# A two-layer mixer kernel: its steps in another order, keys scaled out of PSUM beside the values, small products held among large ones, the output projection begun with the heads' half

## The chip, the cores and the metric

One core of a Trainium2 chip runs the whole program in one launch. The metric is the device time of that launch in microseconds (us). The kernel before was timed three times; the median stands in the table below. Engines: PE is TensorE (PEld its weight loads), DVE is VectorE, ACT is ScalarE, POOL is GpSimd, SP is SyncE, which issues most of the DMAs. PSUM is the memory that PE writes its results to; here it is used in eight banks, two to each of four pools (pi, pa, pb, pc).

## The reference, cut to what matters

Everything is float32. Two layers of 512 tokens by 1024 features, each of four steps:

```python
h <- LN(alpha*h + 0.5*SwiGLU_a(h))
h <- LN(alpha*h + W_o [GDN | SB | MLA](h))     # the mixer
h <- LN(alpha*h + 0.5*SwiGLU_b(h))
h <- h + sigmoid(h W_g) * (p[i] W_p)
```

Only the mixer changes. It multiplies h by one wide in-projection and feeds three groups of heads. GDN (gated delta rule, 8 heads of 64) works in chunks of 64 tokens. For each chunk and head it needs the inverse of a 64 by 64 lower triangular matrix, applied to two right sides:

```python
lhs = strict_lower(einsum(kb, kc) * decay) + eye(C)
u = triangular_solve(lhs, vc * bc)                # values times beta
w = triangular_solve(lhs, kb * exp(gc))           # keys times beta and decay
v_new = u - w @ state;  o = q_dec @ state + qk @ v_new
state = state * g_last + k_dec.T @ v_new
```

The output of GDN is normalised and multiplied by silu of a gate gz. SB (stick-breaking attention, 4 heads) and MLA (latent attention, 4 heads, low-rank queries and keys) are attentions over the 512 tokens. The 1024 features of the three groups go through W_o.

## The kernel before, in words

**Large products.** A float32 product is made of three matmuls on split operands (a high part and a low part, `fp32r`): `mm3`, lines 408 to 410. Each has a full 128 by 128 weight tile and 256, 416 or 512 columns; these are called large here. The weights come by DMA (SP), ACT casts the high part (L78) and POOL or DVE subtracts it to get the low part (L80), three weights ahead.

**Small products.** The chunk algebra uses plain float32 matmuls on small corners of the array: tiles of 16 or 32 rows in the inverse, of 64 rows in the products of a chunk.

**The mixer's steps.** A string of names per layer, `OPT[l]["order"]` (L31 and L35), says in which order the steps are written: `k`, `q`, `v`, `si` are in-projections of 128 columns of keys, queries, values and of the stick heads, `pr` the key products of a chunk pair, `inv0` to `inv2` the inverse of the 16 by 16 corners (on DVE: L928 to L957), `in2` and `in3` the corners joined to 32 and 64 (small products on PE, L970 to L1003), `keys` the transposed keys, `lat_in` the latent in-projection, `lh` the latent heads, `dq` the decayed queries, `uw` the products u and w, `mv` the moves of a chunk, `sc` the scan over chunks, `st` the stick attention, `la` and `lo` the latent attention, `gz` the gate, `on` and `go` its norm and product. A scheduler then sets each engine's queue from this order and from when it takes operands to be ready. Each engine works its queue strictly in order.

**u and w.** `u_w(t)` first multiplies the inverse EA by the values (L1022, 64 columns for each head and chunk), ACT copies u out of PSUM (L1023), POOL scales EA by a number per token (L647), PE multiplies the scaled EA by the keys (L1029), ACT copies w (L1030), and POOL scales the keys (L647 on K). `moves(t)` (L1050 and after) needs w and the scaled keys.

**Values.** `in_values` transposes silu of the convolved values y (L870) and scales them out of PSUM (L871); the convolution is three DVE instructions (L839), the product with silu's second factor one more (L667).

**Output projection.** After all steps, the gate is transposed, and then four groups of 24 large matmuls of 512 columns make the first column half of the output, for which four banks are held; the heads of SB and MLA fill one half of the 1024 input features, GDN's the other.

Of the kernel before, what the change touches and what calls it, by code (L numbers as in the profile page):

```python
# [30 lines left out]
    {"order": "gates_in gates q1 si3 si0 k0 k3 si1 decays si2 q2 st03 st02 k1 st01 q3 k2 st00 q0 scales pr2 pr0 st13 st12 st11 st10 pr3 lw pr1 inv0 inv1 inv2 v1 v0 lat_in in2 v3 v2 keys dm lh0 in3 lh3 dq lh2 qs lh1 uw0 mv0 uw1 mv1 uw2 mv2 uw3 mv3 gz0 gz1 la00 la10 lo0 la01 la11 lo1 mxa sc0 sc1 sc2 sc3 la02 la12 lo2 on0 go0 on1 go1 on2 go2 on3 go3 la03 la13 lo3",  # L31
     "units": "MXl SQK EA KS SPb LO K KT KQ1 GZ MXh KQ0 SVM QT V EU MW MGh MGl SPa IA",
     "out": (2, 1, 0, 3),
# [3 lines left out]
     "out": (2, 1, 0, 3),  # L37
     "eng": {"EAm": "V", "EUm": "V", "gu": "V", "sil_max": "G", "sil_mul": "V", "by_EA": "G", "by_K": "G", "gnw": "G", "gout": "G", "mxlo": "G", "new": "G", "splo": "G", "pscale": "V", "c_sphi": "A", "c_stq": "V", "c_pT1": "V", "c_pT0": "A", "c_mo": "A", "c_K": "V", "c_u": "A", "c_w": "A", "c_o": "A", "c_vm": "A", "c_kv": "V", "c_qv": "A", "c_rv": "A", "c_mqT": "A", "c_QKT": "A", "c_mxhi": "A", "c_gz": "A", "c_kt": "A", "c_sv": "A", "r_lnf": "G", "r_lnm": "G", "r_m": "G", "r_k": "V", "r_o": "V", "lnf_g": "V", "lnf_b": "V", "lnm_g": "G", "lnm_b": "V", "f_T": "V", "f_Tlo": "G", "f_S": "V", "f_Slo": "V", "f_c": "G", "f_S3": "V", "f_T3": "G", "c_pj": "V", "sel": "V", "w_gates": "G", "w_si": "V", "w_k": "G", "w_q": "V", "w_v": "G", "w_lat": "G", "w_gz": "G", "w_o0": "G", "w_o1": "G", "s_gates": "G", "s_si": "V", "s_k": "V", "s_q": "V", "s_v": "G", "s_lat": "V", "s_gz": "G", "s_o0": "V", "s_o1": "V"}},
# [78 lines left out]
def trunk(  # L117
# [249 lines left out]
    def plan_mixer(l):  # L367
# [13 lines left out]
        plans = {"gates_in": p_gates, "lat_in": p_lat, "gz0": lambda: p_gz(0), "gz1": lambda: p_gz(1)}  # L381
# [3 lines left out]
        for st in opt["order"].split():  # L385
            if st in plans:
                plans[st]()
# [18 lines left out]
    def mm3(ps, ah, al, bh, bl, first, last):  # L406

        T.matmul(ps, ah, bh, start=first, stop=False)  # L408
        T.matmul(ps, ah, bl, start=False, stop=False)  # L409
        T.matmul(ps, al, bh, start=False, stop=last)  # L410
# [209 lines left out]
    def mixer(l):  # L620
# [9 lines left out]
        def cols(dst, w):  # L630
            for k in range(KD):
                mm3(dst, w[0][:, k * P:(k + 1) * P], w[1][:, k * P:(k + 1) * P], XH[:, k, :], XL[:, k, :], k == 0, k == KD - 1)

        def col_tile():
            w = W.next()
            ps = ibank()
            cols(ps, w)
            return ps

        def tok_tile(ps, t, ws, n, per):  # L640
            for k in range(KD):
                u, kk = k // per, k % per
                mm3(ps, XH[:, k, t * P:(t + 1) * P], XL[:, k, t * P:(t + 1) * P],
                    ws[u][0][:, kk * n:(kk + 1) * n], ws[u][1][:, kk * n:(kk + 1) * n], k == 0, k == KD - 1)
# [32 lines left out]
        KS, LO, Vt = U["KS"], U["LO"], U["V"]  # L677
# [59 lines left out]
        def in_latent():  # L737
            ws = [W.next() for _ in range(4)]
            for t in range(NT):
                ps = ibank()  # L740
                tok_tile(ps[:, 0:416], t, ws, 416, 2)
                CP["kt"](KT[:, t, 0:416], ps[:, 0:416])
# [56 lines left out]
        lo = {}  # L799

        def latent(h2, qt):
            N = (qt + 1) * P
            if qt not in lo:
                lo[qt] = slab("lo", 256)
            for hp in range(2):
# [6 lines left out]
                p_, pT = (MW[:, hp, :N], MW[:, 2 + hp, :N]) if h2 == 0 else (SVM[:, hp, :N], SQK[:, 2 + hp, :N])  # L812
# [50 lines left out]
        def in_values(ct):  # L863
            if True:
                y, e = slab("y"), slab("e")
                conv(col_tile(), 8 + ct, y)
                silu(y, e)
                pv = bank()
                for t in range(NT):
                    T.transpose(pv[:, t * P:(t + 1) * P], y[:, t * P:(t + 1) * P], ident)  # L870
                V.tensor_tensor(out=Vt[:, :, ct * P:(ct + 1) * P].rearrange("p t (h d) -> p t h d", h=2), in0=pv.rearrange("p (t h d) -> p t h d", t=NT, h=2),  # L871
                                in1=th(brk)[:, :, 2 * ct:2 * ct + 2].unsqueeze(3).broadcast_to([P, NT, 2, 64]), op=ALU.mult)
# [17 lines left out]
        def decayed_queries():  # L890
# [3 lines left out]
            eh, el = LO[:, 2, :], LO[:, 3, :]  # L894
            sel = tp.tile([P, 512], F32R, tag="t", name=nm("sel"))
# [68 lines left out]
        def inverse32():  # L964
            DN, QZ = inv_s["DN"], inv_s["QZ"]
            pq = bank()
            for n in range(32):
                for q in range(4):
                    R, o = quad(q)
                    T.matmul(pq[R, n * 16:(n + 1) * 16], LC[R, n, :], DT[R, n, 16:32], start=True, stop=True)  # L970
            A.copy(QZ[:, :, 16:32], pq.rearrange("p (n i) -> p n i", i=16))
            pe_, pn = bank(), one()
            for n in range(32):
                for q in (1, 3, 0, 2):
                    R, K16 = slice(32 * q, 32 * q + 32), slice(32 * q, 32 * q + 16)
                    T.matmul(pe_[R, n * 16:(n + 1) * 16], DN[K16, n, :], QZ[K16, n, 16:32], start=True, stop=True)
                    if q % 2 == 0:
                        T.matmul(pn[R, n * 16:(n + 1) * 16], QZ[K16, n, :], DN[K16, n, 0:16], start=True, stop=True)
# [7 lines left out]
        def inverse64():  # L986
            DN, TS = inv_s["DN"], inv_s["QZ"]
            pt = banks()
            for n in range(32):
                for cp in range(2):  # L990
                    R = slice(cp * 64 + 32, cp * 64 + 64)
                    T.matmul(pt[n // 16][cp * 64:cp * 64 + 32, (n % 16) * 32:(n % 16) * 32 + 32], EAf[R, n, 0:32], EAf[R, n, 32:64], start=True, stop=True)
# [7 lines left out]
            for n in range(32):  # L1000
                for cp in range(2):
                    R = slice(cp * 64, cp * 64 + 32)
                    T.matmul(py[n // 16][R, (n % 16) * 32:(n % 16) * 32 + 32], DN[R, n, :], TS[R, n, :], start=True, stop=True)  # L1003
# [6 lines left out]
        def keys():  # L1010
            for ct in range(4):
                pk = bank()
                for t in range(NT):
                    T.transpose(pk[:, t * P:(t + 1) * P], kq(ct, 0)[:, t * P:(t + 1) * P], ident)
                CP["K"](K[:, :, ct * P:(ct + 1) * P], pk.rearrange("p (t c) -> p t c", t=NT))

        def u_w(t):
            pu = bank()
            for hh in range(8):
                for cp in range(2):  # L1020
                    R = slice(cp * 64, cp * 64 + 64)
                    T.matmul(pu[R, hh * 64:(hh + 1) * 64], EA[R, t, hh * 64:(hh + 1) * 64], Vt[R, t, hh * 64:(hh + 1) * 64], start=True, stop=True)  # L1022
            CP["u"](Vt[:, t, :], pu)  # L1023
            by_token(EN["by_EA"], EA[:, t, :], EA[:, t, :], cw2, t)
            pw = bank()
            for hh in range(8):
                for cp in range(2):
                    R = slice(cp * 64, cp * 64 + 64)
                    T.matmul(pw[R, hh * 64:(hh + 1) * 64], EA[R, t, hh * 64:(hh + 1) * 64], K[R, t, hh * 64:(hh + 1) * 64], start=True, stop=True)  # L1029
            CP["w"](EA[:, t, :], pw)  # L1030
            by_token(EN["by_K"], K[:, t, :], K[:, t, :], kd, t)
# [10 lines left out]
        def moves(t):  # L1042
            pa = banks()
            for hh in range(8):
                h2, hp = hh // 2, hh % 2
                for cp in range(2):
                    R = slice(cp * 64, cp * 64 + 64)
                    Rh, c = slice(hp * 64, hp * 64 + 64), slice(hh * 64, (hh + 1) * 64)
                    for w_, rhs in ((0, K), (1, EU)):
                        T.matmul(pa[cp][Rh, w_ * 256 + h2 * 64:w_ * 256 + (h2 + 1) * 64], EA[R, t, c], rhs[R, t, c], start=True, stop=True)  # L1050
# [5 lines left out]
            for cp in range(2):  # L1056
                R = slice(cp * 64, cp * 64 + 64)
                pb = bank()
                for hh in range(8):
                    h2, hp = hh // 2, hh % 2  # L1060
                    T.matmul(pb[hp * 64:hp * 64 + 64, h2 * 64:(h2 + 1) * 64], K[R, t, hh * 64:(hh + 1) * 64], Vt[R, t, hh * 64:(hh + 1) * 64], start=True, stop=True)
# [259 lines left out]
```

## Time and profile before

| | us |
|---|---|
| median of three runs | 2320.2 (2308.31 to 2324.55) |
| the profiled execution | 2316.84 |
| its span | 2315.1 |
| PE busy | 2254.1 (97%) |
| DVE, ACT, POOL busy | 1310.1 (57%), 1059.9 (46%), 854.9 (37%) |

The profile is of one execution. The two mixers run from about 370 to 765 us and from about 1520 to 1910 us of its span. In a row of a timeline the first number is the start, the second the time in the engine. Matmuls are pipelined: how long one keeps PE is read from the start of the next, not from its own second number. In rows of plain float32 products, one product of the program shows as two instructions. PEclk is the clock granted to PE as a share of the full 2.4 GHz; the lower level is 1.2 GHz.

### The profile page before, as it was taken

How to read it: one execution, taken by the hardware profiler on the slowest of the kernel's cores; microseconds unless marked ns; L12 is line 12 of the kernel's file. 1: busy time of each engine (PE TensorE's matmuls, PEld its weight loads, DVE VectorE, ACT ScalarE, POOL GpSimd, SP SyncE). 2: the span in 40 equal slices, each digit the busy share in tenths (PEclk: the TensorE clock that was granted, in tenths of full speed). 3: DMA queues.
4: the chain of work that ended last, by engine and by line, in shares of the span. 5: the costliest groups of instructions: out<-in, count | busy, mean ns of one | idle time of the engine just before them, and what ended most of it. 6: DMA issues, size and time to landing. Idle time of an engine off the chain costs nothing.

```text
span 2315.1 us, 41403 instructions
## 1 busy us (share of the span) xinstructions
PE 2254.1 (97%) x17362; PEld 2001.4 (86%) x17362; DVE 1310.1 (57%) x1988; ACT 1059.9 (46%) x1751; POOL 854.9 (37%) x467
## 2 busy tenths in 40 slices
PE   8999999999989999999999999999999899999999
PEld 8999888767777999988889998887687789999887
DVE  7777416655435877642567774165553558777233
ACT  5555423653443555532345554236535445556222
POOL 4222452432334422255432225524334244223442
PEclk9999999998899999999999999999999899999999
DMA  5332342212103233234313323422120033333331
GB/s 170 101 105 91 115 125 63 60 38 59 47 21 89 76 110 101 82 119 128 122 44 108 101 93 110 128 56 67 37 77 23 20 92 97 104 102 98 112 101 64
DMA packets 186795, 199.94 MB, mean 86 GB/s; under 512 B 10128, under 2 KB 151536, under 8 KB 186608
## 3 DMA queue, kind: packets, MB, share of 16 engines
q1 hardware_dynamic: 186608, 197.29, 28.2%
q8 instruction: 136, 2.23, 0.4%
q14 instruction: 51, 0.42, 0.1%
HBM read 195.17 MB, written 2.10 MB: 85 GB/s over the span
## 4 chain that ended last, share of the span: by engine, by line
PE 90%; DVE 4%; POOL 2%; issue 2%; ACT 1%; DMA 1%; SPq 0%; POOLq 0%; DVEq 0%; ACTq 0%
PE pi L408 6%; PE pi L409 6%; PE pi L410 6%; PE pc L414 4%; PE pc L416 4%; PE pc L415 4%; PE pa L416 3%; PE pa L415 3%; PE pa L414 3%; PE pb L416 3%; PE pb L415 3%; PE pb L414 3%; PE pb L408 3%; PE pb L410 3%; PE pc L410 3%; PE pc L408 3%
## 5 line engine op out<-in xcount | busy, mean ns | idle before, releaser
L80 POOL TENSOR_TENSOR wlo<-wraw,whi 128x1024 fp32r<-128x1024 f32 (+4 forms) x169 | 351.5, 2089 | 407.7 <-ACT whi L78 399.6
L78 ACT CAST whi<-wraw 128x1024 fp32r<-128x1024 f32 (+2 forms) x162 | 167.0, 1033 | 346.0 <-PE pa L410 166.1
L100 POOL TENSOR_TENSOR wlo<-wq,whi 128x1024 fp32r<-128x1024 f32 x48 | 121.4, 2529 | 291.6 <-ACT whi L99 291.6
L99 ACT CAST whi<-wq 128x1024 fp32r<-128x1024 f32 x116 | 121.7, 1049 | 131.8 <-issue 37.7
L100 POOL TENSOR_TENSOR wlo<-wraw,whi 128x1024 fp32r<-128x1024 f32 x32 | 82.2, 2568 | 234.6 <-ACT whi L99 186.5
L99 ACT CAST whi<-wraw 128x1024 fp32r<-128x1024 f32 x84 | 88.1, 1049 | 96.2 <-issue 25.8
L414 PE MATMUL pb<-x,whi 128*128 128x256 f32 x448 | 127.0, 286 | 2.5 <-ACT x L255 1.7
L415 PE MATMUL pb<-x,whi 128*128 128x256 f32 x448 | 127.3, 286 | 0.0
L414 PE MATMUL pc<-x,whi 128*128 128x256 f32 x448 | 126.8, 283 | 0.4 <-ACT sg L184 0.4
L100 DVE TENSOR_TENSOR wlo<-wq,whi 128x1024 fp32r<-128x1024 f32 x68 | 84.5, 1243 | 75.4 <-ACT whi L99 75.4
L416 PE MATMUL pb<-x,wlo 128*128 128x256 f32 x448 | 127.1, 286 | 0.0
L415 PE MATMUL pc<-x,whi 128*128 128x256 f32 x448 | 126.8, 283 | 0.0
L416 PE MATMUL pc<-x,wlo 128*128 128x256 f32 x448 | 126.7, 283 | 0.0
L99 ACT CAST whi<-s 128x1024 fp32r<-128x1024 f32 x80 | 83.9, 1049 | 69.5 <-PE pc L415 40.1
L100 DVE TENSOR_TENSOR wlo<-s,whi 128x1024 fp32r<-128x1024 f32 x80 | 106.8, 1335 | 0.0
L409 PE MATMUL pi<-x,whi 128*128 128x512 f32 x256 | 104.9, 410 | 0.7 <-issue 0.7
L410 PE MATMUL pi<-x,wlo 128*128 128x512 f32 x256 | 104.4, 408 | 0.0
L408 PE MATMUL pi<-x,whi 128*128 128x512 f32 x256 | 104.2, 407 | 0.0
L100 DVE TENSOR_TENSOR wlo<-wraw,whi 128x1024 fp32r<-128x1024 f32 x52 | 65.6, 1261 | 57.1 <-ACT whi L99 57.1
L416 PE MATMUL pa<-x,wlo 128*128 128x256 f32 x320 | 91.8, 287 | 2.8 <-DVE wlo L100 2.8
L414 PE MATMUL pa<-x,whi 128*128 128x256 f32 x320 | 91.5, 286 | 0.0
L415 PE MATMUL pa<-x,whi 128*128 128x256 f32 x320 | 91.5, 286 | 0.0
(575 smaller groups left out, 7698.2 us busy)
## 6 DMA issues: line engine op xcount, KB each, us to landing
wq<-in_ffa_w_in_dram SPq DMA_DIRECT2D x46, 512.0 KB, 3.7
wq<-in_ffb_w_in_dram SPq DMA_DIRECT2D x46, 512.0 KB, 3.8
wraw<-in_ffa_w_out_dram SPq DMA_DIRECT2D x44, 512.0 KB, 3.7
wraw<-in_ffb_w_out_dram SPq DMA_DIRECT2D x44, 512.0 KB, 3.7
wraw<-in_mix_w_in_dram SPq DMA_DIRECT2D x40, 512.0 KB, 3.8
wraw<-in_ffa_w_in_dram SPq DMA_DIRECT2D x34, 512.0 KB, 3.6
wraw<-in_ffb_w_in_dram SPq DMA_DIRECT2D x34, 512.0 KB, 4.0
wraw<-in_mix_w_o_dram SPq DMA_DIRECT2D x16, 512.0 KB, 3.7
```

The source lines that it names most:

```text
L78: self.nc.scalar.copy(hi[:, :width], raw[:, :width])
L80: (eng or self.nc.gpsimd).tensor_tensor(out=lo[:, c], in0=raw[:, c], in1=hi[:, c].bitcast(F32), op=ALU.subtract)
L99: nc.scalar.copy(hi, q[name])
L100: eng(name).tensor_tensor(out=lo, in0=q[name], in1=hi.bitcast(F32), op=ALU.subtract)
L408: T.matmul(ps, ah, bh, start=first, stop=False)
L409: T.matmul(ps, ah, bl, start=False, stop=False)
L410: T.matmul(ps, al, bh, start=False, stop=last)
L414: T.matmul(dst, ah, bhl[:, 0], start=first, stop=False, skip_group_check=True)
L415: T.matmul(dst, ah, bhl[:, 1], start=False, stop=False, skip_group_check=True)
L416: T.matmul(dst, al, bhl[:, 0], start=False, stop=last, skip_group_check=True)
```

## The change

The order string of both layers is new; `pr` and the inverse come right after `scales`, all four `v` come before `in2`, and the latent in-projection is cut into `lat0` to `lat3`, of 24 large matmuls each. A step written `in2~lat0,lat1` is woven: the function of the small products yields after each of its 64 groups, and a large matmul of the named steps, from the seventh on, is ordered behind a group in proportion (no semaphore, an order for the scheduler only). `gz0 gz1` come before `uw0`.

`keys` makes the transposes by token tile and evicts each bank twice, scaled: once into VK beside the values, once into K. `u_w` then needs one stage: EA times (value, scaled key) pairs of 128 columns. Values are scaled out of PSUM in two instructions in place of one. The gate has its tiles in the two tags of the layer norm's parameters, so the loads of these (`ln_load`) come behind the gate's transposes. Of the output projection the half on the heads of SB and MLA comes ahead of the gate's transposes, and the first half's banks are two of pi, and one each from two other calls.

```diff
-"... st00 q0 scales pr2 pr0 st13 st12 st11 st10 pr3 lw pr1 inv0 inv1 inv2 v1 v0 lat_in in2 v3 v2 keys dm lh0 in3 lh3 dq lh2 qs lh1 uw0 mv0 uw1 mv1 uw2 mv2 uw3 mv3 gz0 gz1 la00 ..."
+"... q0 scales pr2 pr0 pr3 pr1 inv0 inv1 inv2 st00 si3 si1 v1 st13 v0 st12 v2 st11 v3 st10 lw in2~lat0,lat1 keys dm lh0 in3~lat2,lat3 dq lh1 gz0 gz1 uw0 mv0 lh2 qs uw1 mv1 lh3 uw2 mv2 uw3 mv3 la00 ..."
...
-                CP["K"](K[:, :, ct * P:(ct + 1) * P], pk.rearrange("p (t c) -> p t c", t=NT))
+                by_token(V, VK[t][:, 1, :], pk, cw2, t)
+                by_token(V, K[:, t, :], pk, kd, t)
...
-            CP["u"](Vt[:, t, :], pu)
-            by_token(EN["by_EA"], EA[:, t, :], EA[:, t, :], cw2, t)
...
-            CP["w"](EA[:, t, :], pw)
-            by_token(EN["by_K"], K[:, t, :], K[:, t, :], kd, t)
+            for i in range(2):
+                pu = bank()
...
+                        T.matmul(pu[R, hh * P:(hh + 1) * P], EA[R, t, c], VK[t][R, :, c], start=True, stop=True)
+                CP["w" if i else "u"](VK[t][:, :, i * 256:(i + 1) * 256].rearrange("p w (h d) -> p h w d", h=4), pu.rearrange("p (h w d) -> p h w d", h=4, w=2))
...
+        def woven(gen, fill):
+            n, done = sum(96 if f[:2] == "gz" else 24 for f in fill), [0]
+            small_ = []
+            def turn(i):
+                done[0] += 1
+                if done[0] > 6 and (done[0] - 6) * 64 // n < len(small_):
+                    tc.add_manual_dep(i.ins, small_[(done[0] - 6) * 64 // n].ins.name, NOSYNC, reason="among the small products")
+                while len(small_) < 64 and len(small_) * n < done[0] * 64:
+                    small_.append(next(gen))
...
-        ps0 = banks4()
+        ps0 = [ibank(), ibank(), one(True), one(True)]
         ws = [W.next() for _ in range(4)]
         for t in range(NT):
             for i in range(2):
                 mm_o(ps0[t], t, order[i], ws[i], i == 0, False)
+        regroup("silu_and_others")
...
+        ln_load(l, 1)
...
-        pb = banks() + banks(True)
+        pb = banks() + [bank(), bank()]
```

The pieces below are of the engines' queues; a name's number tells buffers apart, `x128` is so many instructions in a row.

PE, layer 1, the first products of `in2` (`pa<-IA`) with the large matmuls about them (`pi`: before those of a value step, 512 columns; in the change those of `lat0`). Before:

```order
L408 MATMUL pi_5450<-x_3498,whi_4992 128x512
L970 MATMUL pa_5112<-IA_3702 32x16 x128
L409 MATMUL pi_5450<-x_3498,whi_4992 128x512
L410 MATMUL pi_5450<-x_3498,wlo_4993 128x512
L408 MATMUL pi_5498<-x_3498,whi_4998 128x512
```

In the change:

```order
L410 MATMUL pi_5108<-whi_4991,x_3498 128x416
L975 MATMUL pa_5110<-IA_3702 32x16 x4
L408 MATMUL pi_5108<-whi_4991,x_3498 128x416
L975 MATMUL pa_5110<-IA_3702 32x16 x8
L409 MATMUL pi_5108<-wlo_4992,x_3498 128x416
L975 MATMUL pa_5110<-IA_3702 32x16 x4
```

One block of 128 has become groups of 4 or 8 with a single large matmul between; `in3` looks the same. In layer 1 small products of the inverse follow a large matmul at 78 places of the new queue and at 4 of the old one.

DVE, layer 1, the end of the corners' inverse (`IA`, `DN`) and what stands about it. Before:

```order
L945 TENSOR_TENSOR IA_3702<-pr_4832,pa_4833 128x30
L946 TENSOR_TENSOR pa_4833<-pa_4833,IA_3702 128x2x15
L956 STREAM_TRANSPOSE IA_3702<-X_4872 128x32x32
L957 STREAM_TRANSPOSE DN_4876<-X_4872 128x32x32
L839 SCALAR_TENSOR_TENSOR y_5442<-pi_5450,cw_3678,y_5442 128x511
```

In the change:

```order
L950 TENSOR_TENSOR IA_3702<-pr_4579,pa_4580 128x30
L1111 COPY KS_3685<-pb_4865 64x128
L1113 TENSOR_TENSOR KS_3685<-pb_4865,KS_3685 64x128
L1095 SCALAR_TENSOR_TENSOR SVM_3693<-pc_4949,SVM_3693 128x384
L951 TENSOR_TENSOR pa_4580<-pa_4580,IA_3702 128x2x15
L961 STREAM_TRANSPOSE IA_3702<-X_4619 128x32x32
L962 STREAM_TRANSPOSE DN_4623<-X_4619 128x32x32
L666 TENSOR_TENSOR y_4987<-y_4987,e_4988 128x512
```

The convolutions of the values and the masks and copies of the stick attention now stand within the inverse, and the last value tile (`y_4987`) is finished only behind its two transposes. On PE the transposes of that tile (`L874 MATMUL pa_5030`) stand ahead of all products of `in2`.

PE, layer 1, the first `u_w`, its second stage before:

```order
L410 MATMUL pi_6417<-whi_5446,x_3498 128x256
L772 MATMUL pc_5756<-SQK_3683,MW_3698 128x384 x2
L773 MATMUL pc_5757<-SVM_3694,MW_3698 128x512
L1029 MATMUL pa_5915<-K_3688,EA_3684 64x64 x16
L408 MATMUL pi_6417<-whi_5446,x_3498 128x256
```

In the change, all of it:

```order
L410 MATMUL pi_6055<-whi_5825,x_3498 128x256
L1033 MATMUL pa_6088<-VA_3695,EA_3684 64x128 x8
L1033 MATMUL pa_6098<-VA_3695,EA_3684 64x128 x8
L770 MATMUL pc_6193<-ident,KT_3689 128x128 x3
L1053 MATMUL pb_6108<-K_3688,VA_3695 64x64
```

The gate's large matmuls (`pi`, 256 columns) stood before, between and behind the stages of `u_w` and `moves`; now all 192 of them stand ahead of it, in one stretch with a few others.

## Rows read from the trace of the kernel before

**Rows 1.** The page: busy time of PE, its share, its instructions.
```profile
PE 2254.1 (97%) x17362; PEld 2001.4 (86%) x17362; DVE 1310.1 (57%) x1988; ACT 1059.9 (46%) x1751; POOL 854.9 (37%) x467
```
**Rows 2.** Windows: length; busy PE, PEld, DVE, ACT, POOL; PEclk; DMA; GB/s.
```profile
527.00:552.50 25.50, 25.50 (x126) 21.76 (x125) 18.82 (x46) 11.41 (x17) 8.12 (x5) 1.00 0.15 42
552.50:595.00 42.50, 35.87 (x991) 31.38 (x991) 18.21 (x30) 10.84 (x20) 16.95 (x11) 0.74 0.22 68
595.00:650.00 55.00, 53.31 (x685) 43.58 (x684) 18.77 (x71) 29.86 (x74) 21.36 (x19) 0.95 0.10 33
650.00:676.00 26.00, 19.72 (x370) 17.05 (x371) 7.50 (x24) 11.93 (x34) 12.74 (x11) 0.80 0.16 43
676.00:719.00 43.00, 36.73 (x363) 29.88 (x362) 27.51 (x102) 19.23 (x45) 8.37 (x7) 0.92 0.01 1
1702.00:1740.00 38.00, 32.63 (x1010) 27.70 (x1008) 19.47 (x38) 13.41 (x29) 17.16 (x12) 0.91 0.31 95
1740.00:1794.00 54.00, 49.73 (x643) 40.50 (x645) 18.90 (x64) 27.24 (x64) 24.04 (x21) 0.94 0.07 21
1794.00:1820.00 26.00, 23.06 (x409) 19.73 (x403) 8.50 (x27) 12.71 (x37) 10.39 (x9) 0.80 0.12 43
1820.00:1862.00 42.00, 35.73 (x356) 29.28 (x356) 27.72 (x98) 18.36 (x43) 8.34 (x7) 0.92 0.00 1
```
**Rows 3.** Waits of PE, 550 to 720 us: us in total, times, longest.
```profile
PE pb L1050 <- POOL K L647: 4.3, 2, 3.1
PE pa L976 <- issue: 3.2, 2, 2.3
```
**Rows 4.** Waits of PE, 1700 to 1862 us.
```profile
PE pa L1029 <- POOL EA L647: 3.2, 2, 2.0
```
**Rows 5.** Timeline of PE about the small products L992.
```profile
577.65 0.28 PE L410 MATMUL pi<-whi,x 128*128 128x256 f32 x1
577.77 0.28 PE L408 MATMUL pi<-whi,x 128*128 128x256 f32 x1
577.98 2.21 PE L992 MATMUL pb<-EA 32*32 32x32 f32 x128
580.12 0.38 PE L409 MATMUL pi<-wlo,x 128*128 128x256 f32 x1
580.35 0.28 PE L410 MATMUL pi<-whi,x 128*128 128x256 f32 x1
```
**Rows 6.** Timeline of PEld at the same place.
```profile
577.98 2.10 PEld L992 LDWEIGHTS pb<-EA 32*32 32x32 f32 x128
580.12 0.19 PEld L409 LDWEIGHTS pi<-wlo,x 128*128 128x128 f32 x1
```
**Rows 7.** Timeline of PE in the stick attention and a value step.
```profile
503.06 0.91 PE L1086 MATMUL pc<-SQK 64*128 64x384 f32 x2
503.90 0.33 PE L1087 MATMUL pc<-sb_neg,id_r 128*128 128x128 f32 x1
...
504.35 0.39 PE L410 MATMUL pi<-x,wlo 128*128 128x512 f32 x1
504.58 0.39 PE L408 MATMUL pi<-x,whi 128*128 128x512 f32 x1
```
**Rows 8.** Timeline of DVE at the end of the inverse.
```profile
546.93 2.14 DVE L956 STREAM_TRANSPOSE IA<-X 128x1024 f32<-128x1024 f32 x1 [2.62 <-ACT X L953]
```
**Rows 9.** Lines L839, L667, L1092, L1023: durations in ns min/median/max.
```profile
L839 DVE SCALAR_TENSOR_TENSOR y<-pi,cw,y x12: 736/748/752, 493.1 to 579.8; 128x511 f32<-128x511 f32 x4, 128x510 f32<-128x510 f32 x4, 128x509 f32<-128x509 f32 x4
L667 DVE TENSOR_TENSOR y<-y,e x4: 682/692/693, 501.5 to 584.3; 128x512 f32<-128x512 f32 x4
L1092 DVE SCALAR_TENSOR_TENSOR SVM<-pc,SVM x8: 280/416/558, 432.8 to 508.9; 128x128 f32<-128x128 f32 x4, 128x384 f32<-128x384 f32 x4
L1023 ACT COPY V<-pa x8: 567/586/590, 607.2 to 1804.5; 128x512 f32<-128x512 f32 x8
```
**Rows 10.** DMA issues: KB each, median us to landing.
```profile
lnb<-in_ln_b_dram SPq DMA_DIRECT2D x6, 512.0 KB, 4.4
```

More of the change, by code (lines that the diff above doesn't have):

```diff
@@ L404, in trunk, with mm3 @@
         plan_ple(l)
[L406 to L410, printed above, removed]
+    def mm3(ps, ah, al, bh, bl, first, last, each=lambda i: None):
+        each(T.matmul(ps, ah, bh, start=first, stop=False))
+        each(T.matmul(ps, ah, bl, start=False, stop=False))
+        each(T.matmul(ps, al, bh, start=False, stop=last))
     def mm2(dst, ah, al, bhl, first, last):
@@ L628, in heads @@
             return s.rearrange("p (h d) -> p h d", h=n)
-        def cols(dst, w):
-            for k in range(KD):
-                mm3(dst, w[0][:, k * P:(k + 1) * P], w[1][:, k * P:(k + 1) * P], XH[:, k, :], XL[:, k, :], k == 0, k == KD - 1)
+        each = [lambda i: None]
         def col_tile():
@@ L636, in col_tile @@
             ps = ibank()
-            cols(ps, w)
+            for k in range(KD):
+                mm3(ps, w[0][:, k * P:(k + 1) * P], w[1][:, k * P:(k + 1) * P], XH[:, k, :], XL[:, k, :], k == 0, k == KD - 1, each[0])
             return ps
@@ L734, in decays, with in_latent @@
                 EN["EUm"].tensor_tensor(out=ev, in0=ev, in1=tri_u.unsqueeze(1).broadcast_to([P, 8, 64]), op=ALU.mult)
[L737 to L742, printed above, removed]
+        lat_ws = []
+        def in_latent(t):
+            lat_ws.extend(W.next() for _ in range(0 if lat_ws else 4))
+            ps = ibank()
+            tok_tile(ps[:, 0:416], t, lat_ws, 416, 2)
+            CP["kt"](KT[:, t, 0:416], ps[:, 0:416])
         wuq = SQK[:, 2:4, :].rearrange("p a b -> p (a b)")
@@ L796, in latent_heads @@
                 CP["QKT"](dst[0:96, t, :], pp[0:96, :])
-        lo = {}
+        lo, old = {}, []
         def latent(h2, qt):
+            if not old:
+                old.append(xp.tile([P, 2, KD, S], F32, tag="x", name=nm("old")).rearrange("p a b s -> p (a b) s"))
             N = (qt + 1) * P
@@ L811, in latent @@
                 V.tensor_reduce(out=mn, in_=s[:, :N], op=ALU.min, axis=AX.X)
-                p_, pT = (MW[:, hp, :N], MW[:, 2 + hp, :N]) if h2 == 0 else (SVM[:, hp, :N], SQK[:, 2 + hp, :N])
+                p_, pT = (old[0][:, (h2 * 2 + qt % 2) * 4 + 2 * i + hp, :N] for i in range(2))
                 act(p_, s[:, :N], AF.Exp, scale=-1.0, bias=mn, accum_out=su)
@@ L969, in inverse32 @@
                     R, o = quad(q)
-                    T.matmul(pq[R, n * 16:(n + 1) * 16], LC[R, n, :], DT[R, n, 16:32], start=True, stop=True)
+                    i = T.matmul(pq[R, n * 16:(n + 1) * 16], LC[R, n, :], DT[R, n, 16:32], start=True, stop=True)
+                yield i
             A.copy(QZ[:, :, 16:32], pq.rearrange("p (n i) -> p n i", i=16))
@@ L1002, in inverse64 @@
                     R = slice(cp * 64, cp * 64 + 32)
[L1003 removed]
+                    i = T.matmul(py[n // 16][R, (n % 16) * 32:(n % 16) * 32 + 32], DN[R, n, :], TS[R, n, :], start=True, stop=True)
+                yield i
             for n in range(2):
@@ L1147, in scan_norm, with gz @@
             V.tensor_tensor(out=heads(o), in0=heads(o), in1=of.unsqueeze(2).broadcast_to([P, 8, 64]), op=ALU.mult)
-        GZ = U["GZ"]
+        GZ = []
+        def gz(t):
+            if not GZ:
+                GZ.extend(x.rearrange("p (t c) -> p t c", t=2)[:, i, :] for x in (lnp.tile([P, 1024], F32, tag=n, name=nm("gz")) for n in ("lnb", "lng")) for i in range(2))
+            return GZ[t]
         def in_gz(n):
@@ L1190, in mixer @@
                 steps[f"la{h2}{t}"] = lambda h2=h2, t=t: latent(h2, t)
-        for st in opt["order"].split():
-            steps[st]()
-        regroup("silu_and_others")
-        for t in range(NT):
-            pp = bank()
-            for ct in range(4):
-                T.transpose(pp[:, ct * P:(ct + 1) * P], GZ[:, t, ct * P:(ct + 1) * P], ident)
-            split_from_psum(MGh[:, :, t * P:(t + 1) * P], MGl[:, :, t * P:(t + 1) * P], pp.rearrange("p (c s) -> p c s", c=4))
-        ln_load(l, 1)
+        def woven(gen, fill):
[7 more added lines that the diff above has]
+                    small_.append(next(gen))
+            each[0] = turn
+            for f in fill:
+                steps[f]()
+            each[0] = lambda i: None
+            for _ in gen:
+                pass
+        for st in opt["order"].split():
+            if "~" in st:
+                woven(steps[st.split("~")[0]](), st.split("~")[1].split(","))
+            else:
+                steps[st]()
         def mm_o(ps, t, u, w, first, last):
@@ L1216, in mixer @@
                 mm_o(ps0[t], t, order[i], ws[i], i == 0, False)
+        regroup("silu_and_others")
+        for t in range(NT):
+            pp = bank()
+            for ct in range(4):
+                T.transpose(pp[:, ct * P:(ct + 1) * P], gz(t)[:, ct * P:(ct + 1) * P], ident)
+            split_from_psum(MGh[:, :, t * P:(t + 1) * P], MGl[:, :, t * P:(t + 1) * P], pp.rearrange("p (c s) -> p c s", c=4))
+        ln_load(l, 1)
         for t in range(NT):
```

78 lines of the change are left out of this document (38 added, 40 removed), and 6 rows, old and new, of the table OPT.

## The prediction

> **What bounds the kernel now.** I read the page first: PE is busy for 97% of the span [rows 1], so time can only be won where PE stands idle, where its clock is down, or where its own work shrinks. Next come windows by stage [rows 2], because the change touches the mixers alone. In each window I take two losses: the idle time (length less busy PE) and the clock (length times one less PEclk). In layer 1 the stretch of `in2` and `in3` (552.5 to 595) loses 6.6 idle and 11.1 by the clock, 17.7 us. The stretch of the latent heads, `uw` and `mv` (two windows, 595 to 676) loses 8.0 and 8.0, that of the scan, the latent attention and the start of the output projection (676 to 719) 6.3 and 3.4. In layer 2 the same three lose 5.4 and 3.4, 7.2 and 8.4, 6.3 and 3.4. All of it is 43.4 and 34.1 us, 77 us in both layers; nothing that the change does can win more than that, unless it makes PE's own work less. The window ahead of `in2` (527 to 552.5) loses nothing: 25.50 busy of 25.50, clock 1.00.
>
> The waits of PE say what the idle time is. In layer 1 the largest is for POOL's scaling of the keys, 4.3 us, and in `in2` 3.2 us stand as "issue", which is no other engine [rows 3]; in layer 2 the scaling of EA leads with 3.2 us [rows 4].
>
> Then the timeline where small products meet large ones, because the change makes many more such places [rows 5]. Large matmuls of 256 columns start 0.12 us apart (577.65 to 577.77). The last one ahead of the small block holds PE for 0.21 (577.77 to 577.98), the first behind it for 0.23 (580.12 to 580.35). So going in costs 0.09 us more, and coming out at least 0.11.
>
> **The change, term by term** (both layers; times against the profiled execution of 2316.8 us).
>
> *Alternations.* The new queue has 78 places per layer where small products of the inverse follow a large matmul, the old one 4: 74 more. The starts give 0.20 us for each [rows 5]. Some time is spent also before 580.12, in the last small product, whose end the large weights may have to await; no row separates it, and I allow up to 0.10, as much as on either edge that is seen. The other bound is zero: a group of 4 or 8 might be loaded and run under a streaming large matmul, which a block never shows. I take 0.23, near the rows: 17 us per layer, **+34**, bounds 0 and +44.
>
> The Trainium skill ("TensorE: Matmul & The Clock Gate", Part 3, The mechanism) says that a weight load overlaps matmuls in flight only when it goes to other row groups. A full-height large load shares row groups with every small product, so by that rule the case of hidden alternations (a rival below) could not be, and its chance would go to the forecast. The edges in [rows 5] agree with the rule; a large load takes 0.19 us [rows 6], about the 0.20 that they show. No row here shows a group of 4 between two large matmuls, so I keep the rival.
>
> *Waits in the woven stretch.* PE's queue has the transposes of the last value tile ahead of `in2`, and DVE finishes that tile only behind both transposes of the inverse. From the end of the key products to there DVE has its 18.8 us of before in the window 527 to 552.5 [rows 2], and new within it nine convolutions of 0.75, four products of 0.69, nine more masks and copies of the sticks of about 0.42 [rows 9] and about 0.7 for values evicted in halves: 18.8 + 6.7 + 2.8 + 3.8 + 0.7 = 32.8, and the wait for ACT of 2.6 [rows 8], 35.4 us. PE has in the same stretch 65 matmuls of 512 columns at 0.23 (504.35 to 504.58) [rows 7], 15.0; six of 416 at 0.19 (scaled), 1.1; and 52 stick products, masks and transposes, the longest of them 0.84 (503.06 to 503.90) [rows 7], taken at 0.25, 13: 29 us. It waits for 6, since the large matmuls that could fill are held behind small products that come later. Bounds: 0 (DVE does part of it earlier), 12 (at half the time for the 52). Three hand-overs follow inside `in2` and `in3` (first to second products through an ACT copy, 0.59 for one such [rows 9], and to `in3` through DVE), each now with large matmuls held: 1.3 each with the way there and back, 4 in all, bounds 2 and 8. So 10 us idle where 6.6 and 5.4 stood; the "issue" wait goes with the blocks.
>
> *The clock in that stretch.* Before, PEclk was 0.74 over 42.5 us in layer 1 and 0.91 over 38 in layer 2 [rows 2]. The stretch grows to some 65 us of half-filled PE. I take 5 us, between the two losses of before and nearer the smaller, as the solid blocks are gone; bounds 0 and 17 (0.74 over 65 us).
>
> The stretch then loses 10 + 5 + 17 = 32 where 17.7 and 8.8 were lost: 14 and 23, **+37**.
>
> *`uw` and `mv`.* One stage less: the waits for POOL go, with them its sixteen scalings, eight DVE copies become sixteen scaled ones (DVE is busy 18.8 of 55 us there [rows 2], so they cost nothing; without that cover each is 0.69). The small matmuls halve in number and double in columns: zero. Late next are ACT's copies, 0.59 each [rows 9], with little to cover them, since the gate's large matmuls stand ahead. I take 3 us idle per layer and 6 of clock (small products with no large ones about them, a little better than the 8 before): 31.6 becomes 18, **-13.6**. Bounds: 0 (ACT takes POOL's place, its queue holds the weights' casts) and -26.
>
> *Scan, latent attention, output.* 48 large matmuls of the heads' half, 11 us, become free to fill. Idle 6.3 becomes 1.5, clock 3.4 becomes 1: 19.4 becomes 5, **-14.4**, bounds -5 and -19.
>
> *Tail.* The layer norm's loads now wait for the gate's transposes, in SP's queue behind weights. They land 4.4 us after issue [rows 10] and are wanted after the second half's products; with a thinner cover, 12 large matmuls of 2.8 us, I charge 1.5 per layer, **+3**, bounds 0 and +9.
>
> *Moved steps ahead of `in2`* cost nothing: that window is full now and has the same large matmuls to fill; if DVE falls behind there, it is the wait charged above.
>
> **Sum:** 34 of alternations is within the 37; 37 - 13.6 - 14.4 + 3 = +12, 2329 for the profiled execution. The median stands 3.4 us above it, so 2332.
>
> **The rivals.**
>
> *The clock stays down in the woven stretch (slower).* Place: from the first group of `in2` to the last of `in3`. For it: in layer 1 the clock was 0.74 just there, and a wait of 6 us stands ahead. Against it: 0.91 in layer 2, and 0.92 in the scan's window, where PE is busy 36.7 of 43 [rows 2]. Price: 17 in place of 5 per layer, +24, so 2356. It decides from a loss of 10.7 per layer on (another 5.7), where 2332 passes 2343.
>
> *The alternations are hidden and DVE keeps up (faster).* If a small group costs only its own products under a large one that streams, with some 0.05 left for each of the 148 places, 27 us go; without the wait for the value tile 12 more: 2332 - 39 = 2293. For it: the small products are short, and the block's edges are the only rows. Against it: both edges of the block show the cost.
>
> *`uw` wins nothing (ACT in POOL's place).* ACT casts weights in the same queue. Then 2332 + 13.6 = 2346.
>
> *The weaving does not hold:* the queue shows it does, so this gets no chance of its own.
>
> **Chances.** Forecast 0.45 (its own range 2316 to 2345), slow clock 0.20, hidden alternations 0.25, `uw` 0.10. A difference of under 1% is taken as no change: 2297 to 2343. The hidden case lies mostly below 2297, and a little is left for more gain in `uw` and the output than I charged: faster 0.25. Slow clock and half of the `uw` case, with the upper edge of the forecast: slower 0.29. Same 0.46. The range runs from 2287, which takes in most of the hidden case, to 2361 for the slow clock.
>
> **What the profile after would show.** Right: single large matmuls of 416 columns between small groups with starts 0.28 or more apart; a wait of some 6 us of PE for DVE at the value transposes (L874); no waits for POOL in `u_w` and `moves`; few gaps in the scan. Wrong: starts of 0.19 to 0.2 through the groups (then the hidden case); PEclk under 0.8 over the woven stretch (slow clock); PE waiting for ACT at L1053 (the `uw` case). My sum fails most easily in the 0.23 per place, where a tenth of a microsecond is 15 us.

## The result, and the profile after

The change made the kernel slower: 2414.9 us (median of 4 runs, 2407.2 to 2420.1) against 2319.6 before (4 runs by then), a ratio of 1.041 with a 95% interval of 1.038 to 1.045. I had forecast 2332, with 2361 as the upper end, so the sign was open in my text and the size was missed. The page of the changed kernel, its busy times and the clock in 40 slices of the span:

```profile
PE 2355.0 (98%) x17106; PEld 2034.9 (84%) x17106; DVE 1337.2 (55%) x2004; ACT 1056.2 (44%) x1751; POOL 851.7 (35%) x451
...
PEclk9999999996799999999999999999758999999999
```

PE is busy for 101 us more than in [rows 1], with 256 instructions fewer. The clock has two dents, one in each mixer. The windows of the changed kernel (columns as in [rows 2]), cut by stage: in layer 1 from the first product of `in2` to the last of `in3`, then `u_w` and `mv`, the scan with the latent attention, and the output projection; last, `in2` to `in3` in layer 2:

```profile
532.80:634.00 101.20, 100.99 (x1057) 60.46 (x1057) 20.05 (x49) 17.38 (x37) 17.80 (x12) 0.60 0.08 23
...
664.00:699.00 35.00, 29.98 (x579) 24.29 (x579) 15.12 (x43) 20.44 (x52) 12.88 (x10) 0.90 0.10 33
699.00:746.00 47.00, 46.36 (x492) 36.94 (x482) 24.68 (x86) 21.68 (x60) 11.60 (x9) 1.00 0.12 35
746.00:792.00 46.00, 40.19 (x205) 32.75 (x205) 28.36 (x64) 15.20 (x22) 20.84 (x14) 0.93 0.33 103
1730.40:1835.00 104.60, 104.39 (x1056) 62.15 (x1056) 19.98 (x49) 17.32 (x37) 17.79 (x12) 0.57 0.07 23
```

The woven stretch takes 101 and 105 us. PE hardly idles there (0.2 us), and its clock is 0.60 and 0.57: by length times one less PEclk, 40 and 45 us are lost by the clock. That measure takes all work to run at half speed at the lower level; the turns shown below lose 0.36 of their time there, which would make it 29 and 32. Where [rows 2] showed gaps, this shows a slow PE. The reader should not take "PE 98%" for a better kernel.

Not all of that stands behind a gap. In layer 1 the clock is down first from 529 to 540 us, about the wait of 2.5 us at L874 and some shorter gaps ahead of it; it then stood at full for 13 us of woven work and fell again with PE recorded busy all the time:

```profile
540.00:553.00 13.00, 13.00 (x169) 6.96 (x167) 2.41 (x6) 1.75 (x4) 1.27 (x1) 1.00 0.06 21
553.50:563.50 10.00, 10.00 (x115) 6.99 (x119) 0.00 (x0) 0.99 (x2) 0.00 (x0) 0.50 0.00 0
```

In layer 2 it fell ahead of the stretch, at 1724 us among gaps of 0.2 to 0.4 us, and came back for a first short spell at 1768.

The starts in the two profiled executions tell where the 99 us of span went (us; the gate's large matmuls, 23 us a layer, and the latent in-projection's, 18 us, have moved, so single lines mix moved work with lost time; the sum doesn't):

| from, to | layer 1 before, after | layer 2 before, after |
|---|---|---|
| first product of `gates` (L708) to first of `in2` | 163.4, 146.0 | 158.6, 145.8 |
| first of `in2` to last of `in3` | 39.8, 100.3 | 30.2, 103.5 |
| last of `in3` to first of the next FFN | 167.1, 159.0 | 170.0, 157.4 |
| all outside these | 1586.0, 1602.2 (both layers) | |

The first two lines together are 43 and 60 us worse, the third 8 and 13 better, the last 16 worse.

**A place of the weaving.** The timeline of PE in the woven stretch at full clock:

```profile
548.66 0.46 PE L409 MATMUL pi<-wlo,x 128*128 128x416 f32 x1
549.05 0.25 PE L975 MATMUL pa<-IA 32*32 32x16 f32 x8
549.23 0.46 PE L410 MATMUL pi<-whi,x 128*128 128x416 f32 x1
```

and where the clock is down:

```profile
611.70 0.32 PE L1011 MATMUL pb<-QZ,DN 32*32 32x32 f32 x4
611.95 0.71 PE L409 MATMUL pi<-wlo,x 128*128 128x416 f32 x1
612.59 0.32 PE L1011 MATMUL pb<-QZ,DN 32*32 32x32 f32 x4
612.84 0.71 PE L410 MATMUL pi<-whi,x 128*128 128x416 f32 x1
```

A turn with the same number of `in3`'s products, in a short spell at full clock:

```profile
606.04 0.25 PE L999 MATMUL pb<-EA 32*32 32x32 f32 x4
606.22 0.46 PE L410 MATMUL pi<-whi,x 128*128 128x416 f32 x1
606.61 0.25 PE L999 MATMUL pb<-EA 32*32 32x32 f32 x4
```

A single large matmul between two groups holds PE for 0.39 us (548.66 to 549.05); in a row of its kind it is 0.19 (shown with e2 below). A group of 8 instructions holds it for 0.18 (549.05 to 549.23); of a block of 36, also shown with e2, 8 take 0.09. So a place costs 0.20 + 0.09 = 0.29 us at the full clock, and one turn takes 0.57. At 1.2 GHz a turn with 4 of `in3` is 0.89 (611.70 to 612.59), and at full clock 0.57 (606.04 to 606.61): the lower clock adds 0.32, which is 0.36 of the longer turn. A large matmul of 0.19 and four small ones at 2.14 / 128 us each [rows 5] would take 0.26 undisturbed at full clock: the place costs 0.31 more there, and place and lower clock together 0.63.

**The waits.** PE's waits in the changed kernel that are new or longer than before:

```profile
PE pa L263 <- DVE h L320: 10.1, 2, 5.6
PE pc L796 <- DVE MW L792: 9.5, 2, 5.0
...
PE pa L874 <- DVE y L666: 2.8, 2, 2.5
```

POOL's scalings of [rows 3, 4] are gone. In their place stand the latent heads (L796), late next behind DVE, and the end of the mixer (L263, the transposes of the next x). The value tile (L874), which I had put at 6 us a layer, costs 2.5 in layer 1 and 0.3 in layer 2; before, the value tiles cost 2.0 in all. The end, in PE's timeline:

```profile
776.40 0.60 PE L263 MATMUL pa<-ident,h 128*128 128x128 f32 x4
776.91 0.66 PE L263 MATMUL pi<-ident,h 128*128 128x128 f32 x4
783.17 1.09 PE L263 MATMUL pa<-ident,h 128*128 128x128 f32 x4 [5.60 <-DVE h L320]
783.91 0.78 PE L408 MATMUL pa<-w,MXh 128*128 128x512 f32 x1
```

Products of the third token tile (783.91, into a bank of `pa`) stand behind transposes of the second, which wait for DVE's norm; and after the 5.6 us of idle they run at half clock.

### The profile page after: what moved, and what is told of

Same layout as the page of the kernel before. It is cut to its first block, busy times and chain, and to the rows that moved or that the text cites. A ratio compares the mean times of both kernels' runs of the same rounds, so it can differ in the third digit from the quotient of the medians.

```text
span 2414.3 us, 40897 instructions
## 1 busy us (share of the span) xinstructions
PE 2355.0 (98%) x17106; PEld 2034.9 (84%) x17106; DVE 1337.2 (55%) x2004; ACT 1056.2 (44%) x1751; POOL 851.7 (35%) x451
## 4 chain that ended last, share of the span: by engine, by line
PE 91%; DVE 5%; DMA 1%; ACT 1%; issue 1%; POOL 1%; SPq 0%; DVEq 0%; POOLq 0%; ACTq 0%
PE pi L410 7%; PE pi L408 7%; PE pi L409 7%; PE pc L416 4%; PE pc L415 4%; PE pc L414 4%; PE pa L416 3%; PE pb L415 3%; PE pa L415 3%; PE pa L414 3%; PE pb L416 3%; PE pb L414 3%; PE pc L408 2%; PE pb L408 2%; PE pb L410 2%; PE pb L409 2%
## 5 line engine op out<-in xcount | busy, mean ns | idle before, releaser
L100 POOL TENSOR_TENSOR wlo<-wraw,whi 128x1024 fp32r<-128x1024 f32 x32 | 85.5, 2671 | 233.4 <-ACT whi L99 185.2
L100 DVE TENSOR_TENSOR wlo<-wq,whi 128x1024 fp32r<-128x1024 f32 x68 | 91.6, 1347 | 70.9 <-ACT whi L99 70.9
L408 PE MATMUL pi<-x,whi 128*128 128x512 f32 x256 | 103.3, 404 | 2.7 <-DVE KQ L843 2.7
L409 PE MATMUL pi<-x,whi 128*128 128x512 f32 x256 | 100.8, 394 | 0.0
L408 PE MATMUL pi<-whi,x 128*128 128x256 f32 (+2 forms) x256 | 96.0, 375 | 0.0
L410 PE MATMUL pi<-whi,x 128*128 128x256 f32 (+2 forms) x256 | 95.3, 372 | 0.0
```

The costliest lines, as they stand in the source:

```text
L100: eng(name).tensor_tensor(out=lo, in0=q[name], in1=hi.bitcast(F32), op=ALU.subtract)
L408: each(T.matmul(ps, ah, bh, start=first, stop=False))
L409: each(T.matmul(ps, ah, bl, start=False, stop=False))
L410: each(T.matmul(ps, al, bh, start=False, stop=last))
```

## The experiments

Ratios are to the kernel before, run beside each on the same chip, with 95% intervals. Differences between two runs are taken from their ratios. One per cent is 23 us.

**The weaving undone (e1).**

```diff
-"... in2~lat0,lat1 keys dm lh0 in3~lat2,lat3 dq ..."
+"... lat0 lat1 in2 keys dm lh0 lat2 lat3 in3 dq ..."
```

> The change with the weaving alone undone: the small products of in2 and in3 are written as plain steps behind lat0 lat1 and lat2 lat3, with no order between small and large; all else of the change stands. Theory A (the weaving is the loss: each of 78 places per layer costs about 0.3 us at full clock, and the half-filled stretch holds the clock at 1.2 GHz): about 90 to 105 us come back, to 2310 to 2325, and PEclk over in2 and in3 is back over 0.75. Rival B (the wait of PE for the last value tile, which DVE finishes late, starts the low clock, and the lost time follows from that): the wait stays, so at most 30 us come back, to 2385 or more. Rival C (PE's work in the stretch is that long in any form): no change within 10 us.

Measured: 2309.5 us, 0.9972 (0.9951 to 0.9992), some 102 us less than the change. The windows of the same stretch:

```profile
538.00:588.00 50.00, 46.39 (x1038) 36.33 (x1036) 25.16 (x49) 18.74 (x38) 19.26 (x12) 0.90 0.19 58
...
1678.50:1731.00 52.50, 45.94 (x1036) 36.32 (x1036) 28.46 (x50) 18.51 (x38) 19.23 (x12) 0.87 0.20 55
```

102.5 us in both layers where the change has 205.8. Of the 103 us between them some 12 are moved work: the change's stretch holds 84 more matmuls of 416 columns at 0.19 and 37 fewer of 256 at 0.12. The clock is 74 by length times one less PEclk (85.5 less 11.8), or some 53 at the 0.36 of the turns. With 10 us less idle, 28 to 48 are left for the places at full-clock price; 148 more of them at 0.29 would be 43. Theory A holds, but how the loss divides between clock and places is known only so far. Since e1 has also lost the wait at L874, B is not refuted by e1 alone.

**The weaving alone (e4).**

```diff
-v1 v0 lat_in in2 v3 v2 keys dm lh0 in3 lh3 dq
+v1 v0 v3 v2 in2~lat0,lat1 keys dm lh0 in3~lat2,lat3 lh3 dq
...
+        def woven(gen, fill):
```

> The kernel before with the weaving alone (all four values ahead of in2, the latent in-projection in four parts, small products of in2 and in3 held among them); keys, u_w, gate and output projection as before. Theory A: the weaving alone costs 90 to 110 us, so about 2410 to 2430. If the loss comes from the weaving together with the new keys, the moved gate or the earlier key products, less than half of it shows here: under 2370.

Measured: 2440.0 us, 1.0538 (1.0395 to 1.0682) by two runs: +125 us, with an interval of 91 to 158. No other part of the change is needed for the loss. The windows of the stretch in its profile:

```profile
550.80:638.50 87.70, 87.48 (x1024) 53.92 (x1025) 13.75 (x29) 13.40 (x26) 14.06 (x9) 0.58 0.04 14
1752.40:1844.00 91.60, 91.39 (x1024) 55.95 (x1025) 13.74 (x29) 13.52 (x26) 14.06 (x9) 0.54 0.05 13
```

**Eight groups for 64 (e2).** Same large matmuls, held in the same proportion, fewer places: 15 per layer in its trace, where the change has 78.

```diff
-                yield i
+                if n % 8 == 7:
+                    yield i
...
-                if done[0] > 6 and (done[0] - 6) * 64 // n < len(small_):
+                if done[0] > 6 and (done[0] - 6) * 8 // n < len(small_):
```

> The change with 8 groups of small products per step in place of 64: still woven and held among the same large matmuls, but the places where small follow large fall to about an eighth. Theory A1 (each place costs, by itself and through the clock): most of the 100 us of the woven stretch come back, to 2325 to 2345. Rival A2 (holding large matmuls back is what costs, whatever the size of a group): under 25 us come back, 2390 or more.

Measured: 2332.4 us, 1.0083 (1.0063 to 1.0103), some 76 us less than the change. The end of a small block (36 instructions in 0.42 us) and large matmuls in a row in its timeline, and the windows of its stretch:

```profile
551.83 0.48 PE L975 MATMUL pa<-IA 32*32 32x16 f32 x36
552.25 0.45 PE L409 MATMUL pi<-wlo,x 128*128 128x416 f32 x1
552.54 0.35 PE L410 MATMUL pi<-whi,x 128*128 128x416 f32 x1
552.73 0.35 PE L408 MATMUL pi<-whi,x 128*128 128x416 f32 x1
552.92 0.35 PE L409 MATMUL pi<-wlo,x 128*128 128x416 f32 x1
```

```profile
533.00:593.00 60.00, 58.81 (x1056) 44.13 (x1055) 20.59 (x50) 17.09 (x36) 15.81 (x12) 0.82 0.07 22
1691.00:1753.00 62.00, 60.99 (x1057) 45.63 (x1057) 20.72 (x50) 17.20 (x37) 16.21 (x12) 0.78 0.08 21
```

Starts are 0.19 us apart again from the second on (552.54 to 552.73), and the clock is at 0.82 and 0.78. The number of places makes most of the loss, 76 of 102 us. PE still waits for the value tile here (2.3 us in all), so that wait doesn't bring the long spell: as the main cause, theory B falls. A spell of lower clock does stand about that wait. At the start of `in2` the clock is down in e2, with PE idle at times, and up in e1, which has no such wait (e2, then e1, each in layer 1 and 2):

```profile
527.00:541.00 14.00, 11.61 (x74) 6.57 (x73) 8.08 (x12) 10.83 (x22) 3.79 (x4) 0.51 0.10 28
1684.00:1705.00 21.00, 20.28 (x123) 11.64 (x122) 8.74 (x14) 12.17 (x25) 5.07 (x5) 0.51 0.07 20
...
532.00:560.00 28.00, 26.46 (x601) 17.91 (x599) 9.02 (x19) 13.13 (x27) 4.08 (x4) 1.00 0.09 26
1672.00:1700.00 28.00, 26.18 (x596) 17.95 (x596) 9.46 (x20) 13.21 (x27) 4.08 (x4) 1.00 0.10 26
```

In layer 1 it fell at 527 us and the longest idle time, 2.0 us at L874, ended at 532: the wait did not start the spell. The 26 us by which e2 stays above e1 are left to this spell, to the holding and to the 15 places; no run divides them.

**More large matmuls between the groups (e3).**

```diff
-in2~lat0,lat1 keys dm lh0 in3~lat2,lat3 dq lh1 gz0 gz1 uw0
+in2~lat0,lat1,lat2,lat3 keys dm lh0 in3~gz0,gz1 dq lh1 uw0
```

> The weaving over more large matmuls: in2 among lat0 to lat3 (96 large matmuls), in3 among gz0 and gz1 (192 of 256 columns), in place of 48 and 48; about as many groups, with 1.5 and 3 large matmuls between two. If the count of places decides (0.3 us each at full clock, and the clock falls with it), the time stays within 15 us of the change's 2415. If the share of time that large matmuls stream decides the clock, the clock recovers in part and 40 us or more come back, to 2375 or less.

Measured: 2381.3 us, 1.0284 (1.0125 to 1.0444) by two runs only (2368.7 and 2393.8), some 30 us less than the change, but with an interval of 37 either way: between the two expectations, so it decides neither. Its stretch in layer 1 has 69 places and holds some 6 of the gate's 23 us as well; below its row stand two parts of `in2` and one of `in3`:

```profile
532.60:630.00 97.40, 96.85 (x1114) 62.44 (x1114) 21.75 (x51) 19.72 (x41) 20.18 (x13) 0.71 0.10 30
...
569.00:578.00 9.00, 9.00 (x175) 5.77 (x174) 0.00 (x0) 0.29 (x1) 0.00 (x0) 1.00 0.01 4
580.00:594.00 14.00, 14.00 (x163) 8.47 (x163) 0.00 (x0) 3.13 (x3) 6.66 (x3) 0.50 0.27 78
597.00:618.00 21.00, 21.00 (x123) 16.07 (x123) 8.06 (x17) 1.42 (x6) 6.88 (x4) 0.50 0.10 34
```

The clock is 0.71 in place of 0.60 with almost as many places, which speaks for what lies between them. But neither explains it alone: within `in2` the clock falls at about 579, with PE recorded busy, and the turns on either side of the fall are the same, groups of 12 with one or two large matmuls between. It stays down through the places of `in3`, where three of 256 columns stand between.

**The output projection alone (e7), and with the old banks (e12).**

```diff
-      "out": (2, 1, 0, 3),
+      "out": (3, 2, 1, 0),
...
+        ps0 = [ibank(), ibank(), one(True), one(True)]
...
-        pb = banks() + banks(True)
+        pb = banks() + [bank(), bank()]
```

e12 is the same without the last two lines: it keeps `banks(True)`.

> The kernel before with the output projection's part alone: order (3, 2, 1, 0), heads' half ahead of the gate's transposes, new banks. My prediction charged -14.4 us to it: about 2300. Rival: the scheduler puts the 48 matmuls behind the latent attention anyway, or the held banks of pi and pc stop others: within 5 us of 2315, or slower.

> e7 (the kernel before with the new output projection) with the second half's banks as before (pb, pc). If the pa banks make the loss of e7, it comes back to 2310 to 2320; if the heads' half taken early is what leaves too few matmuls for the end, it stays within 6 us of e7's 2337.

Measured: e7 2336.6 us, 1.0094 (1.0064 to 1.0124); e12 2314.1 us, 1.0000 (0.9979 to 1.0021), as expected for the banks. So the second half's banks cost 22 us, and the heads' half, which I had put at -14.4, wins nothing in the old order. PE's wait at L263 for the norm, 8.1 us in e7, is not among the waits of e12, nor of the kernel before:

```profile
PE pa L263 <- DVE h L320: 8.1, 2, 4.1
```

**The old banks in the unwoven version (e10), and the old output projection (e11).**

```diff
-        pb = banks() + [bank(), bank()]
+        pb = banks() + banks(True)
```

> The unwoven version (e1) with the second column half's last two sums in the pc banks, as before, in place of pa, which the transposes of the next x need too. Theory: in e7 and e1 the span outside the mixers is 15 to 21 us longer than before, since the products of t=2 stand behind transposes that wait for DVE's norm (5.6 us of idle and a half-clock spell per layer); with the banks apart they fill that wait, 10 to 18 us less than e1: 2291 to 2299. Rival: the first half's sums hold the pc banks as long, or the late lng holds the norm: within 4 us of 2309.

> The unwoven version (e1) with the output projection of the kernel before (order 2 1 0 3, nothing ahead of the gate's transposes, banks pi and pa, then pb and pc); new keys, new order and the gate in the norm's tags stay. If the output part as a whole costs (e7: about 22 us), 15 to 25 us less than e1: 2284 to 2294, the best so far. If the gate in the norm's tags is what makes the end late, the norm's loads stay late and it is within 6 us of e1.

The edit is e10's, on e1; e11 has the whole output projection of before there. Measured: e10 2280.4 us, 0.9860 (0.9841 to 0.9878); e11 2291.4 us, 0.9905 (0.9888 to 0.9921). e11 is where it was expected. e10 beats both kernels, by more than I expected. Its timeline at the end:

```profile
724.16 0.40 PE L410 MATMUL pc<-w,MGl 128*128 128x512 f32 x1
725.39 0.63 PE L263 MATMUL pa<-ident,h 128*128 128x128 f32 x4 [0.83 <-DVE h L320]
725.77 0.48 PE L408 MATMUL pc<-w,MGh 128*128 128x512 f32 x1
```

The products of the third tile, now in `pc`, run while DVE makes the norm; the wait is 0.83 in place of 5.60. The late load of the norm's parameters (`lng`) stays as it was, so it was not what cost the end. With the right banks the output projection is worth 10 us in the new order (e10 against e11).

**The gate in another unit (e5), and the latent heads ahead of the gate (e6, e13).**

```diff
-            return GZ[t]
+            return KS[:, t, :]
...
-dq lh1 gz0 gz1 uw0 mv0 lh2 qs uw1 mv1 lh3 uw2 mv2 uw3 mv3
+dq lh1 lh2 qs lh3 gz0 gz1 uw0 mv0 uw1 mv1 uw2 mv2 uw3 mv3
```

The first two lines, on e1, are e5; the order is changed on top of e5 (e6) and on e10 (e13).

> The unwoven version (e1) with the gate kept in the unit KS, which the stick attention has left by then, in place of the layer norm's two tags, so the norm's parameters and the weights behind them are no longer held in SP's queue. Theory: in the change PE waits 5 to 6 us per layer for DVE's norm behind the late lng (landing about 3.5 us after its issue behind the last gate transpose), and the weights behind it are late as well; the stretch from the output to the next steps was 8.6 and 10.3 us longer than before, so about 17 to 20 us come back: 2288 to 2294. Rival: DVE and the products' order make the norm late by themselves, and the load was never last: within 5 us of e1's 2309.

> As e5, with the latent heads lh2, qs and lh3 ahead of the gate and of u_w (as in the kernel before) in place of among the chunk products. Theory: PE's waits at L796 for DVE's rope tiles (8 to 9.5 us in both layers, with a half-clock spell of 6.8 us behind each) go, since the gate's large matmuls cover them: 10 to 16 us less than e5, 2273 to 2284. Rival: the waits only move to the next instruction that needs those tiles or ACT's copies of u and w: within 5 us of e5.

> e10 with the latent heads lh2, qs and lh3 ahead of the gate and u_w. PE waits 6.9 us at L796 and 3.3 us at L770 for DVE in e10, both layers. If the gate's large matmuls cover these waits, 6 to 12 us less than e10: 2268 to 2274. If the heads were what filled u_w's own waits for ACT's copies, as e6 (no gain over e5) suggests, 2278 or more.

Measured: e5 2337.5 us, 1.0091 (1.0068 to 1.0115); e6 2341.0 us, 1.0109 (1.0088 to 1.0130); e13 2289.9 us, 0.9883 (0.9828 to 0.9937). In all three the theory missed; e6 and e13 came out as their rivals said. e5 was to win 17 to 20 us and loses 28 against e1, which its rival (within 5 us) did not say either. Its windows from the last `u_w` to the gate's transposes:

```profile
632.00:704.50 72.50, 64.96 (x543) 48.53 (x538) 34.06 (x118) 31.22 (x91) 11.89 (x11) 0.84 0.05 16
...
1789.50:1867.50 78.00, 70.23 (x571) 53.27 (x564) 37.52 (x127) 32.91 (x93) 15.04 (x12) 0.83 0.07 21
```

and the same part of e1, in layer 1 (its latent heads stand ahead of it):

```profile
644.00:690.00 46.00, 45.73 (x499) 36.67 (x494) 24.31 (x86) 21.91 (x60) 11.22 (x9) 1.00 0.12 36
```

The scheduler set another order there (all chunk products first, then the latent heads bare), and 7.5 us of idle and a clock of 0.84 came with it. Why the place of the gate moved that order I have not found. The heads ahead of the gate don't help either: in e13 PE still waits 7.2 us for DVE at L796.

**The old order with the new keys and the new output (e9).** e5 with the order string of before.

> The change with the step order of the kernel before (latent in-projection in four plain parts, nothing woven), gate in KS; so new keys and u_w and new output projection in the old order. If the new keys win the waits for POOL (8 to 10 us over both layers and some clock) and the output wins as charged, 2288 to 2295; the difference from e7 is the price of keys and u_w, predicted at -13.6. Rival: ACT's copies take POOL's place, within 5 us of e7. Against e6 it shows what the new order is worth without weaving: 10 us or more in favour of e6 if moving the key products and the gate helps.

Measured: 2335.8 us, 1.0090 (1.0064 to 1.0116), against 1.0094 of e7: the expected 13.6 us do not show. But e9 has the gate in KS and e7 has not, and in the new order that alone cost 28 us; PE's new waits of e5 stand in e9 too (4.4 us at L796, 4.2 at L770). So what the new keys and `u_w` are worth in the old order is not shown. Against e6 (1.0109) the new order without weaving shows no gain, but that is with the gate in KS, which both have.

## Why the prediction was wrong

- **The step that failed is "The clock in that stretch".** I took 5 us a layer, with 17 as the upper bound (0.74 over 65 us), because I carried over the clock of the old stretch and took the new one to be 65 us long. Measured: 0.60 over 101 us and 0.57 over 105, which is 40 and 45 us by the prediction's own measure and still 29 and 32 by the turns. The rival of the slow clock named the right place and the right way, but it was priced by the same bound, at 2356; its sign, PEclk under 0.8, came. The error is also one of coupling: a turn with 4 of `in3` takes 0.89 at 1.2 GHz in place of 0.57, so the low clock and the places lengthen the stretch together. I had added the two terms as if each stood alone. Why the clock stays down with PE recorded busy is not shown.
- *Alternations:* 34 us predicted; 0.29 at a place in the timeline in place of 0.23, or 43 for the 148 more places, and 28 to 48 by e1's windows. Right in way, a little small. A large matmul between groups holds PE longer by 0.20, about as long as a large weight load takes (0.19 us, [rows 6]). The rule of the Trainium skill ("TensorE: Matmul & The Clock Gate", Part 3, The mechanism), that a weight load overlaps only matmuls in other row groups, agrees with the 0.39 where 0.19 stood. As it stands it does not fit the rows of large matmuls: they start 0.12 apart [rows 5] with loads of 0.19 [rows 6], so loads do overlap matmuls there that fill the same rows, and the rows decide. The rival of hidden alternations, which the rule spoke against, is refuted by the 0.39 and by e1 and e2.
- *Waits in the woven stretch:* 10 us a layer predicted; 0.2 idle within it and 2.5 at L874. What was to be idle was filled by PE's own slowness.
- *`uw` and `mv`, and the output:* -28 together predicted, -21 measured (third line of the table, into which some 11 us of the gate's matmuls have moved: 92 of them stood before the last of `in3`). The waits for POOL went as said, but 9.5 us at L796 came, of which I had named the kind ("late next") and the wrong engine, ACT. In the old order the output alone wins nothing (e12), and the keys and `u_w` are not priced alone (e9). In the unwoven new order with the old output, e11 stands 22 us under before, and the output adds 10.
- *Tail:* +3 predicted, +16 outside the mixers measured. I had looked at the late load of the norm's parameters; it is the pa banks, 22 us in e7 against e12 and 26 in e1 against e10. From the first product of the FFN behind layer 2's mixer to the end, the profiles have 412.6 us before, 422.9 in the change, 423.1 in e1 and 412.8 in e10. I had seen that only 12 large matmuls stand ahead, and priced the wrong cause.
- By the ratios: the weaving +102, the banks +26, and the rest of the change -32, which is e10.

What stays open: how much of the low clock each of the two things brings, the number of places or the few large matmuls between them (e2 changes the first, e3 mainly the second, and PEclk is higher in both); what makes it fall in the midst of equal turns, as in e3; what the new keys and `u_w` are worth alone; and why the gate's unit changes the order in e5.

## What to carry to other kernels

Interleaving to fill gaps pays only as long as a switch between tile shapes on PE is cheaper than the gap; price the switch from the edges of a block in the trace, count the switches in the new queue, and let the clock's loss grow with them instead of adding it as a constant. A busier PE is not a faster one: compare PE's busy time for the same work, beside the granted clock. And look at which bank a sum is put into: sums that share a pool with the next step's transposes can put both behind the slowest engine.

## What the runs showed of the hardware that I had not expected

A single large matmul between groups of small ones holds PE for 0.39 us where one in a row of its kind holds it for 0.19. The difference is as long as its weight load, and the weight loads' own rows fit: between groups the load starts with its matmul (548.66, in the change), in a row it starts 0.19 ahead of it (552.54 for the one at 552.73, in e2):

```profile
548.66 0.19 PEld L409 LDWEIGHTS pi<-wlo,x 128*128 128x128 f32 x1
...
552.54 0.19 PEld L408 LDWEIGHTS pi<-whi,x 128*128 128x128 f32 x1
```

That the load then stands in the open is read from these starts. And the granted clock stayed at 1.2 GHz through most of two stretches of 101 and 105 us in which the records show PE busy all the time; before, the lowest share of any stretch in [rows 2] was 0.74 over 42.5 us, with 6.6 us of idle time and solid small blocks in it.
